# A weight chunk's products with the upper weights first, then those with the lower ones

## The chip, the cores and the metric

The kernel runs on one core of a Trainium2 chip. The core has TensorE for matrix products, VectorE, ScalarE and GpSimd for element-wise work, and SyncE, which here issues the weights' DMAs. The time of a kernel is the device time of the core in microseconds, from a run without the profiler; it is given as a median of several runs. A profile is one more execution, recorded by the hardware profiler, with its own time and, a little shorter, its span from the first to the last instruction.

## The reference

A decoder trunk of two layers on 256 positions of width 2048, all in float32. Layer A mixes positions by attention over three groups of dilated windows. Layer B is an attention of three branches (compressed, selected and sliding-window keys), whose keys and values come from one shared projection. Behind each mixer stand an output projection, a feed-forward part with squared ReLU and a gated embedding; rmsnorms stand ahead of all of them.

```python
qkv = (xn @ w_in).reshape(B, S, 3, G * Hg, dh)           # mixer A
o   = softmax_over_groups(dilated attention) @ w_out
kv  = (hn @ w_kv).reshape(B, S, 6, G, dh)                # shared by mixer B
k_cmp = gelu(blocks(k) @ w1) @ w2                        # compression; v alike
qg  = xn @ w_qg                                          # mixer B: queries, gates
o   = (g0 * o_cmp + g1 * o_slc + g2 * o_win) @ w_out
h   = relu(xn @ mlp_w1) ** 2;   x = x + h @ mlp_w2       # 2048 -> 8192 -> 2048
x   = x + sigmoid(xn @ ple_w_gate) * (p @ ple_w_proj)
```

Nearly all of the arithmetic is in the products of 256 positions with weights.

## The kernel before

The activations are held feature-major: a tile has 128 features on its partitions and the 256 positions on its columns. The products take their operands in a reduced float32 format (fp32r). To keep the precision, each number is split in two: an upper part, which is the number rounded to that format, and a lower part, which is the rest. A split activation tile is 512 columns wide, with the upper halves of the 256 positions in the first 256 columns and the lower halves in the others. The weights are split on the chip too.

The weights come in 875 chunks of 128 by 1024 numbers. For each chunk SyncE issues a DMA to a raw tile (4 buffers), ScalarE casts it to the upper tile `whi` (line 197, 6 buffers), and VectorE subtracts to get the lower tile `wlo` (line 203, 5 buffers). `Program.run` writes the order out by hand: at each chunk it issues the DMAs up to 7 chunks ahead, the casts and subtractions 3 to 4 chunks ahead, then lets the unfinished evictions (Python generators) advance one step each, and then emits the chunk's products. Each engine's queue takes its instructions in the order in which they are written there.

A chunk holds eight weight tiles of 128 by 128. For each of them `mm_tile` issues two products into one PSUM bank: the upper weights with all 512 columns of the split activation (line 321), which gives upper by upper in the first 256 columns and upper by lower in the others, and the lower weights with the first 256 columns (line 322), which adds lower by upper to the first half. Lower by lower is left out. So each of the eight tiles has a product of 512 columns and one of 256, and each product has its own load of 128 by 128 weights into the array. When a bank is complete its two halves are added (`sum_halves`, a copy on ScalarE at line 326 and an addition on VectorE at line 328), or both are added to the residual stream (lines 437 and 438).

Two functions call `mm_tile`. `quad` makes four output tiles of 128 features at once, in four banks. A chunk covers two blocks of 128 input features for these four tiles; eight chunks complete the quad when there are 2048 input features, four chunks when there are 1024, and one chunk for the embedding's 256. Four banks of the ring `mm` and four of the ring `at` take turns between quads. All of the feed-forward part, the gates, the output projections and the shared keys are quads. `single` makes one output tile in one bank from two chunks of eight input blocks each; the queries and keys of mixer A, the queries of mixer B and the last four gate tiles are singles. The very last one sums in 256 columns only (`one_half`, lines 376 to 378) and does not call `mm_tile`.

Three other forms of large product stand beside these. `token_major` makes the value tiles with the activations as the loaded operand and 512 columns of weights streaming (lines 404 to 406, twelve products of 512 columns in a chunk). `compress` has eight products of 256 columns in a chunk (lines 893 and 894); its chunks take turns with those of a value unit. Sixteen products of 512 columns make the gates of mixer B (line 1036).

Of the kernel before, what the change touches and what calls it, by code (L numbers as in the profile page):

```python
# [15 lines left out]
P = 128  # L16
D = 2048
T = 256
KT = D // P
# [113 lines left out]
def kernel(ctx: ExitStack, tc: tile.TileContext, a: dict, out: bass.AP):  # L133
    nc = tc.nc
# [22 lines left out]
    def bank():  # L157
        return pspool.tile([P, 512], F32, tag="mm", name="mm", bufs=4)
# [156 lines left out]
    def have(acts, k):  # L315
        prog.until(lambda: acts[k] is not None)
        return acts[k]

    def mm_tile(ps, hi, lo, col, rhs, first, last):

        nc.tensor.matmul(ps, hi[:, col:col + P], rhs, start=first, stop=False)  # L321
        nc.tensor.matmul(ps[:, :T], lo[:, col:col + P], rhs[:, :T], start=False, stop=last)  # L322

    def sum_halves(ps):
        s = tmp.tile([P, T], F32, tag="es", name="es", bufs=4)
# [7 lines left out]
    def four_banks():  # L333
        parity[0] ^= 1
        if parity[0]:
            return [bank() for _ in range(4)]
        return [p[:, i, :] for p in (banks2(), banks2()) for i in range(2)]

    def delayed(g, n):
        for _ in range(n):  # L340
            yield
        yield from g

    def quad(src, nk, acts, done, hooks=None, single_ring=False, late=False):

        st = []
        for c in range(nk // 2):
            def step(hi, lo, c=c):
                if c == 0:
                    st.extend([bank() for _ in range(4)] if single_ring else four_banks())  # L350
                for i in range(2):
                    have(acts, 2 * c + i)
                for f in range(4):
                    for i in range(2):
                        k = 2 * c + i
                        mm_tile(st[f], hi, lo, i * 512 + f * P, acts[k], k == 0, k == nk - 1)
                if c < nk // 2 - 1:
                    return []
                return [delayed(done(f, st[f]), f // 2 if late else 0) for f in range(4)]
            prog.chunk(src(c), step)  # L360
            for fn in (hooks or {}).get(c, ()):
                prog.op(fn)

    def single(src, acts, done, mid=(), ring=bank, one_half=False):

        st = []
        for c in range(2):
            def step(hi, lo, c=c):
                if c == 0:
                    st.append(ring())  # L370
                for i in range(8):
                    k = 8 * c + i
                    if one_half:
                        xg, ps = have(acts, k), st[0][:, :T]
                        wh, wl = hi[:, i * P:(i + 1) * P], lo[:, i * P:(i + 1) * P]
                        nc.tensor.matmul(ps, wh, xg[:, :T], start=k == 0, stop=False)
                        nc.tensor.matmul(ps, wh, xg[:, T:], start=False, stop=False)
                        nc.tensor.matmul(ps, wl, xg[:, :T], start=False, stop=k == KT - 1)
                        continue
                    mm_tile(st[0], hi, lo, i * P, have(acts, k), k == 0, k == KT - 1)  # L380
                return [done(st[0])] if c else []
            prog.chunk(src(c), step)
            if c == 0:
                for fn in mid:
                    prog.op(fn)
# [902 lines left out]
```

## Time and profile before

| | us |
|---|---|
| median of 3 runs | 2519.74 (2519.64 to 2519.77) |
| profiled execution | 2519.91 |
| its span | 2518.1 |
| TensorE products, busy | 2507.3 |
| TensorE weight loads, busy | 2204.1 |
| VectorE, busy | 1716.8 |
| ScalarE, busy | 1342.8 |
| DMA, mean rate | 185 GB/s |

In the profile, PE is TensorE, PEld its weight loads, DVE is VectorE, ACT is ScalarE, POOL is GpSimd and SP is SyncE. L321 is line 321 of the kernel. A group of instructions is given by line, engine, operation, the written tile, an arrow and the read tiles, with a count, busy time and the mean length of one in ns, and behind the bar the idle time of its engine just before them with what ended it. Products on TensorE are pipelined and their ends are modelled, so a recorded product is longer than the distance to the next one; starts are what counts. A row of the chain has a start, the time that passed until the next link, and the instruction. A row of the windows has the window, its length, the busy time and number of instructions, the granted clock (1.00 is full), the DMA engines' busy share and the rate in GB/s.

### The profile page before, as it was taken

Reading aid. Unit: us, or ns where it says so; the run is one execution under the profiler, and the core shown is the slowest. Engines: PE = TensorE matmul, PEld = TensorE weight load, DVE = VectorE, ACT = ScalarE, POOL = GpSimd, SP = SyncE. Lnnn points to the kernel's source line nnn. Section 1 sums busy time; section 2 is a strip of 40 time slices with the busy share of each in tenths; the row PEclk is TensorE's granted clock in tenths of the full one; section 3 lists DMA queues with packets and bytes.
Section 4 is the critical chain, followed back from the end, with each engine's and each line's share of the span. In section 5 each row is a group of like instructions: output and inputs, shape, how many; then the busy total and the mean of one; then the engine's idle time right before and its main releaser. Section 6 shows DMA issues by size and latency. Waiting matters only on the chain.

```text
span 2518.1 us, 38042 instructions
## 1 busy us (share of the span) xinstructions
PE 2507.3 (100%) x14457; PEld 2204.1 (88%) x14457; DVE 1716.8 (68%) x3000; ACT 1342.8 (53%) x2152; POOL 10.4 (0%) x24
## 2 busy tenths in 40 slices
PE   9999999999999999999999999999999999999998
PEld 8888888888888888888888889888888888888887
DVE  6766677866565665567787989776556656556777
ACT  6444444554454453455564788655435445445555
POOL 0000000000000000000000000000000000000000
PEclk9999999999999999999999999999999999999999
DMA  7555555555555555555565743455555565555653
GB/s 268 173 180 178 175 161 180 176 188 189 193 188 190 192 190 189 190 191 189 185 199 190 248 155 125 141 191 185 192 190 188 191 191 188 190 192 188 190 185 124
DMA packets 130119, 466.23 MB, mean 185 GB/s; under 512 B 14608, under 2 KB 15888, under 8 KB 129936
## 3 DMA queue, kind: packets, MB, share of 16 engines
q1 hardware_dynamic: 129264, 462.68, 56.8%
q8 instruction: 113, 1.85, 0.3%
q0 software_dynamic: 528, 1.07, 0.2%
q14 instruction: 70, 0.57, 0.1%
q10 hardware_dynamic: 144, 0.07, 0.0%
HBM read 461.65 MB, written 2.10 MB: 184 GB/s over the span
## 4 chain that ended last, share of the span: by engine, by line
PE 99%; DVE 0%; DMA 0%; SPq 0%; ACT 0%; issue 0%; DVEq 0%
PE mm L321 31%; PE at L321 26%; PE mm L322 16%; PE at L322 14%; PE mm L404 1%; PE mm L406 1%; PE mm L405 1%; PE at L406 1%; PE at L404 1%; PE at L405 1%; PE at L1135 0%; PE at L673 0%; PE mm L1159 0%; PE mm L893 0%; PE mm L894 0%; DMA raw<-in_w_v 0%
## 5 line engine op out<-in xcount | busy, mean ns | idle before, releaser
L203 DVE TENSOR_TENSOR wlo<-raw,whi 128x1024 fp32r<-128x1024 f32 (+1 forms) x875 | 1065.5, 1219 | 624.8 <-PE at L322 242.1
L197 ACT CAST whi<-raw 128x1024 fp32r<-128x1024 f32 (+1 forms) x875 | 920.4, 1053 | 914.6 <-PE at L321 409.9
L321 PE MATMUL mm<-xa,whi 128*128 128x512 f32 x2176 | 765.1, 395 | 0.0
L322 PE MATMUL mm<-xa,wlo 128*128 128x256 f32 x2176 | 608.1, 279 | 0.0
L321 PE MATMUL at<-xa,whi 128*128 128x512 f32 x1648 | 573.6, 392 | 0.0
L321 PEld LDWEIGHTS mm<-xa,whi 128*128 128x128 f32 x2176 | 407.8, 187 | 91.9 <-issue 0.4
L322 PE MATMUL at<-xa,wlo 128*128 128x256 f32 x1648 | 461.1, 280 | 0.0
L322 PEld LDWEIGHTS mm<-xa,wlo 128*128 128x128 f32 x2176 | 410.6, 189 | 0.4
L321 PEld LDWEIGHTS at<-xa,whi 128*128 128x128 f32 x1648 | 308.3, 187 | 68.0
L321 PE MATMUL at<-h,whi 128*128 128x512 f32 x1024 | 355.7, 391 | 0.0
L321 PE MATMUL mm<-h,whi 128*128 128x512 f32 x1024 | 355.7, 391 | 0.0
L322 PEld LDWEIGHTS at<-xa,wlo 128*128 128x128 f32 x1648 | 311.3, 189 | 0.1
L322 PE MATMUL mm<-h,wlo 128*128 128x256 f32 x1024 | 286.7, 280 | 0.0
L322 PE MATMUL at<-h,wlo 128*128 128x256 f32 x1024 | 286.7, 280 | 0.0
L321 PEld LDWEIGHTS mm<-h,whi 128*128 128x128 f32 x1024 | 191.5, 187 | 42.0
L321 PEld LDWEIGHTS at<-h,whi 128*128 128x128 f32 x1024 | 191.5, 187 | 42.0
L322 PEld LDWEIGHTS mm<-h,wlo 128*128 128x128 f32 x1024 | 193.5, 189 | 0.0
L322 PEld LDWEIGHTS at<-h,wlo 128*128 128x128 f32 x1024 | 193.5, 189 | 0.0
L328 DVE TENSOR_TENSOR et<-mm,es 128x256 f32<-128x256 f32 x137 | 55.8, 422 | 80.3 <-ACT es L326 78.3
L326 ACT COPY es<-mm 128x256 f32<-128x256 f32 x137 | 48.2, 370 | 66.0 <-PE mm L322 63.0
L328 DVE TENSOR_TENSOR et<-at,es 128x256 f32<-128x256 f32 x103 | 43.5, 423 | 36.8 <-ACT es L326 31.3
L326 ACT COPY es<-at 128x256 f32<-128x256 f32 x103 | 37.8, 370 | 51.8 <-DVE et L328 40.5
(301 smaller groups left out, 2387.8 us busy)
## 6 DMA issues: line engine op xcount, KB each, us to landing
raw<-in_w SPq DMA_DIRECT2D x512, 512.0 KB, 3.5
raw<-in_w_qk SPq DMA_DIRECT2D x96, 512.0 KB, 3.7
raw<-in_w_gate SPq DMA_DIRECT2D x56, 512.0 KB, 3.6
raw<-in_w_kv SPq DMA_DIRECT2D x48, 512.0 KB, 4.2
raw<-in_w_v SPq DMA_DIRECT2D x46, 512.0 KB, 3.6
raw<-in_w_q SPq DMA_DIRECT2D x32, 512.0 KB, 4.4
raw<-in_w_oB SPq DMA_DIRECT2D x32, 512.0 KB, 3.6
raw<-in_w_oA SPq DMA_DIRECT2D x16, 512.0 KB, 3.6
```

The source lines that it names most:

```text
L197: nc.scalar.copy(hi[:, c], t[:, c])
L203: nc.vector.tensor_sub(lo[:, c], t[:, c], f32(hi)[:, c])
L321: nc.tensor.matmul(ps, hi[:, col:col + P], rhs, start=first, stop=False)
L322: nc.tensor.matmul(ps[:, :T], lo[:, col:col + P], rhs[:, :T], start=False, stop=last)
L326: nc.scalar.copy(s, ps[:, :T])
L328: nc.vector.tensor_add(t, ps[:, T:], s)
L404: nc.tensor.matmul(st[j], xh, wh, start=k == 0, stop=False)
L405: nc.tensor.matmul(st[j], xl, wh, start=False, stop=False)
L406: nc.tensor.matmul(st[j], xh, wl, start=False, stop=k == KT - 1)
```

## The change

`mm_tile` becomes `mm_tiles`, which takes the chunk's list of eight weight tiles. It issues the eight products with the upper weights (512 columns each), and then the eight with the lower weights (256 columns each). Within each group the order of the tiles is that of before. `quad` and `single` hand it the list; the last single, `token_major`, `compress` and the gates stay as they are. No product is added or left out, and the sums in each PSUM bank get the same terms in another order.

```diff
-    def mm_tile(ps, hi, lo, col, rhs, first, last):
-        nc.tensor.matmul(ps, hi[:, col:col + P], rhs, start=first, stop=False)
-        nc.tensor.matmul(ps[:, :T], lo[:, col:col + P], rhs[:, :T], start=False, stop=last)
+    def mm_tiles(hi, lo, tiles):
+        for ps, col, rhs, first, last in tiles:
+            nc.tensor.matmul(ps, hi[:, col:col + P], rhs, start=first, stop=False)
+        for ps, col, rhs, first, last in tiles:
+            nc.tensor.matmul(ps[:, :T], lo[:, col:col + P], rhs[:, :T], start=False, stop=last)
...
-                for f in range(4):
-                    for i in range(2):
-                        k = 2 * c + i
-                        mm_tile(st[f], hi, lo, i * 512 + f * P, acts[k], k == 0, k == nk - 1)
+                mm_tiles(hi, lo, [(st[f], i * 512 + f * P, acts[2 * c + i], 2 * c + i == 0, 2 * c + i == nk - 1)
+                                  for f in range(4) for i in range(2)])
...
+                tiles = []
                 for i in range(8):
...
-                    mm_tile(st[0], hi, lo, i * P, have(acts, k), k == 0, k == KT - 1)
+                    tiles.append((st[0], i * P, have(acts, k), k == 0, k == KT - 1))
+                mm_tiles(hi, lo, tiles)
```

In the changed kernel the two products stand on lines 326 and 328.

## The prediction

> **What bounds the kernel now.** I read the page first (busy time, slices, chain), then the windows of the two changed lines, then the chain of work piece by piece where single products can be timed.
>
> ```profile
> PE 2507.3 (100%) x14457; PEld 2204.1 (88%) x14457; DVE 1716.8 (68%) x3000; ACT 1342.8 (53%) x2152; POOL 10.4 (0%) x24
> PEclk9999999999999999999999999999999999999999
> PE mm L321 31%; PE at L321 26%; PE mm L322 16%; PE at L322 14%; PE mm L404 1%; PE mm L406 1%; PE mm L405 1%; PE at L406 1%; PE at L404 1%; PE at L405 1%; PE at L1135 0%; PE at L673 0%; PE mm L1159 0%; PE mm L893 0%; PE mm L894 0%; DMA raw<-in_w_v 0%
> L321 PE MATMUL mm<-h,whi 128*128 128x512 f32 x1024 | 355.7, 391 | 0.0
> L328 DVE TENSOR_TENSOR et<-mm,es 128x256 f32<-128x256 f32 x137 | 55.8, 422 | 80.3 <-ACT es L326 78.3
> L326 ACT COPY es<-mm 128x256 f32<-128x256 f32 x137 | 48.2, 370 | 66.0 <-PE mm L322 63.0
> L203 DVE TENSOR_TENSOR wlo<-raw,whi 128x1024 fp32r<-128x1024 f32 (+1 forms) x875 | 1065.5, 1219 | 624.8 <-PE at L322 242.1
> L197 ACT CAST whi<-raw 128x1024 fp32r<-128x1024 f32 (+1 forms) x875 | 920.4, 1053 | 914.6 <-PE at L321 409.9
> ```
>
> TensorE is the bound: it is busy for 2507 of 2518 us at an undiminished clock, and 87% of the chain is lines 321 and 322, the two that move. The makers of the split weights wait for TensorE to free their buffers, not the reverse: VectorE's subtraction and ScalarE's cast of line 203 and 197 idle mostly on a product of line 322 or 321. So an earlier or later wait on a weight tile is worth little, and what counts is how long TensorE takes from the start of one product to the start of the next.
>
> ```profile
> 0.00:2518.10 2518.10, 2204.75 (x6320) 1.00 0.57 185
> ```
>
> This is the window over the whole span for line 321 alone (busy time, and products in brackets). A wide product's recorded time (391 ns in the group row above) is longer than a pair's spacing, so the busy time is one cover over all unbroken stretches of pairs: 6320 pairs, or 790 chunks of 8, in 2204.75 us. Each of the program's 77 stretches is counted about 0.04 too long (0.39 against 0.35), 3 us together, which leaves 2201 us, or 2.787 us a chunk.
>
> ```profile
> 599.80 0.23 PE mm L321
> ...
> 606.04 0.23 PE at L321
> ```
>
> ```profile
> 40.81 0.23 PE mm L321
> ...
> 44.34 0.24 PE mm L321
> ```
>
> Both are the chain (start, length, product). In the MLP, 18 pairs take 606.04 - 599.80 = 6.24 us: 0.3467 a pair, 2.773 a chunk. In the first head's single tiles 10 pairs take 3.53: 0.353 a pair, 2.824 a chunk, with the same products. The spacing thus has a steady value and a slower one, into which a stretch can fall and stay. Over 790 chunks the clean value gives 2191 us, so some 10 us of the 2201 are slow stretches and slow restarts after other TensorE work.
>
> **The change, part by part.**
>
> What is issued. Nothing is added or removed: the same 6320 products with the upper and 6320 with the lower weights, and one weight load for each, as now (14457 loads for 14457 products). In the built program the instructions of VectorE, ScalarE, GpSimd and SyncE stand in the same order as before, DMAs too; only TensorE's order differs, and two more separate waits stand in its queue. So the sum is about spacing. Before, a chunk alternates 512 and 256 columns wide; after, eight products of 512 are followed by eight of 256, and the next chunk goes back to 512.
>
> Spacing in long rows of one width. The row of pairs is not the only form in this trace.
>
> ```profile
> 79.82 0.23 PE mm L405
> ...
> 85.94 0.23 PE mm L405
> ```
>
> ```profile
> 2498.86 0.12 PE at L376
> ...
> 2499.81 0.12 PE at L378
> ...
> 2501.01 0.12 PE at L376
> ```
>
> Twenty-seven products of 512 of a value unit take 6.12 us: 0.2267 each. Ten products of 256 of the last tile, 2499.81 to 2501.01, take 1.20: 0.120 each. Together 0.3467, the same as a clean pair. So a long row of one width gains nothing and loses nothing against clean alternation: this term is 0.
>
> The turn from one width to the other. Where the compression and a value unit take turns, chunks of eight 256-wide and twelve 512-wide products already alternate, all products one after another:
>
> ```profile
> 1400.58 0.23 PE at L404
> ...
> 1419.15 0.23 PE at L404
> ...
> 1431.04 0.23 PE at L404
> ...
> 1432.20 0.23 PE at L406
> ...
> 1433.79 0.12 PE mm L893
> ...
> 1434.75 0.23 PE at L404
> ```
>
> Twelve wide ones take 2.75 us where 12 x 0.2267 = 2.720; the first five take 1.16 where the steady rate gives 1.133, and from there on they run steadily. Eight narrow ones take 0.96, as 8 x 0.120. Five whole periods, from 1400.58 to 1419.15, take 18.57 us, 3.714 each, so a turn to and fro costs 3.714 - 3.680 = 0.034 us, nearly all in the first five wide products after a turn and at the last. The changed chunk makes exactly this turn once: eight wide are more than the five that are slow, so it pays in full. 790 x 0.034 = +27 us. Bounds: 0 (no such cost in this form) and 0.045 (next row).
>
> The form itself. Only one row of wide products with weights as the loaded operand and activations streaming exists, the gates:
>
> ```profile
> 1460.00 0.23 PE mm L321
> 1460.24 0.12 PE mm L322
> 1460.35 3.71 PE mm L1036 x16
> ```
>
> Sixteen in 3.71 us are 0.232 each: they never reach 0.2267. It stands amid slow pairs (1460.00 to 1460.35 is 0.35 for one and the neighbours are 0.353), so I take the row with the same alternation of widths, the compression's, and keep this one as the upper end.
>
> Slow stretches that go. The turn sets the spacing anew in every chunk, so a slow stretch can't last. Of the 10 us above clean, about half are restarts, which stay: a first pair after transposes has 0.31 between its two products where 0.23 is usual,
>
> ```profile
> 1607.37 0.47 PE L321 MATMUL mm<-ko,whi 128*128 128x512 f32 x1
> 1607.68 0.28 PE L322 MATMUL mm<-ko,wlo 128*128 128x256 f32 x1
> ```
>
> and there are dozens of such restarts. The other half, 5 to 6 us, is replaced by the turn's price. Bounds 0 and 10; I take -6.
>
> Waits. The lower weights' tile is asked for at the ninth product, about 8 x 0.23 - 0.23 = 1.6 us later than now; the upper tile is free 16 x 0.173 - 8 x 0.23, some 0.9 us, sooner. TensorE hardly waits for either now (longest wait on line 203: 0.4 us, once), so 0.
>
> ```profile
> PE at L406 <- DVE wlo L203: 0.4, 1, 0.4
> ```
>
> Evictions. In a quad's last chunk the four banks are now complete at 0.69, 1.39, 2.08 and 2.77 us of the chunk; after, at about 2.1, 2.3, 2.6 and 2.8. Four sums that were spread come in a bunch, and VectorE and ScalarE hold a cast or subtraction behind them. What hides it: those tiles are made three chunks (8 us) ahead, the other four banks serve the next quad, and eight chunks (22 us) pass before a bank returns. Without that cover it would be up to 2 us for a quad, four copies of 0.37 and four adds of 0.42, less what overlaps. In the four quads of one chunk the next quad has eight chunks. A single tile's one bank ends when it did. I take 0.
>
> Activations. The eighth activation of a single tile is needed 7 x 0.12 = 0.8 us earlier; they were split chunks before. 0.
>
> Sum: +27 - 6 = +21 us on the profiled execution, 2519.91 us with a span of 2518.1 (the windows' row above has that span); the median of the runs is 2519.74, 0.2 less. Forecast 2540.5 us, +0.8%. With the two terms at their bounds, 2536 to 2549.
>
> **The rivals.**
>
> Rates add. If the turn costs nothing with weights loaded and activations streaming, a chunk is 8 x 0.2267 + 8 x 0.120 = 2.773, as clean now. For it: the clean rates sum exactly. Against it: the compression's period. Time: 2519.7 less 0 to 6 us for slow stretches, about 2517, no measurable change. The Trainium skill, "TensorE: Matmul & The Clock Gate", section "Back-to-back issue gap", gives a spacing of N/2.4 + 2.5 ns, with no term for order, thus 8 x 215.8 + 8 x 109.2 = 2.600 us a chunk before and after and no change; the trace's clean 2.773 shows that something is missing in it, the turns in the compression that order can matter.
>
> Narrow products run faster after a turn. The first eight of line 376 after the pairs take 2499.81 - 2498.86 = 0.95, 0.01 below the steady rate. If each chunk got that and the wide ones were steady at once: 8 x 0.2267 + 0.95 = 2.763. 790 x (2.763 - 2.773) = -8, with the slow stretches -14: 2506 us. It decides if the wide start costs under 0.01. For it: this one row; against: the eight narrow ones in the compression show 0.96.
>
> Wide products never settle. At the gates' 0.232 a chunk is 8 x 0.232 + 0.96 = 2.816, +0.043 on the clean one: +34 - 6 = +28, 2548 to 2549 us. For: the same operand roles. Against: its slow surroundings.
>
> The bunch of sums delays a cast enough that TensorE waits. 0.5 us on each of 76 or so quads would be 38 us. Against: eight microseconds of lead and VectorE at 68%.
>
> **How the numbers follow.** Turn as in the compression 0.44; rates add 0.22; narrow faster 0.14; never settle 0.16; bunched sums 0.04. A measurement here tells about 0.2% (5 us) from no change: faster than 2514.7, 0.14 + 0.06 of the second case; within, 0.16; slower, 0.44 + 0.16 + 0.04. The range 2509 to 2552 leaves out the case of 2506 and the fourth rival; the forecast's own range is 2536 to 2549.
>
> **What would show it.** Right: in the chain of the MLP, eight wide products after a narrow one take 1.84 to 1.85 us (not 1.81), the next eight 0.96, a chunk 2.80 to 2.81; the cover of line 321's and 328's products grows by some 21 us, all elsewhere unchanged; VectorE and ScalarE keep their busy time. Wrong: a chunk of 2.77 (rates add), of 2.76 or less, or waits of TensorE for line 203 or 197.

## The result and the profile after

The changed kernel takes 2532.06 us (median, 2531.84 to 2532.27) against 2519.76 us for the kernel before in the same comparison: a ratio of 1.0049, interval 1.0038 to 1.0059. It is slower by 12.3 us, as forecast in sign; 2540.5 was forecast, with 2536 to 2549 as the forecast's own range. The profiled execution took 2532.27 us with a span of 2530.5.

The page of the profile after, the lines that answer to those shown of before:

```profile
PE 2518.4 (100%) x14457; PEld 2212.9 (87%) x14457; DVE 1709.0 (68%) x3000; ACT 1337.2 (53%) x2152; POOL 10.5 (0%) x24
PEclk9999999999999999999999999999999999999999
L203 DVE TENSOR_TENSOR wlo<-raw,whi 128x1024 fp32r<-128x1024 f32 (+1 forms) x875 | 1064.4, 1218 | 579.2 <-PE at L328 219.5
L197 ACT CAST whi<-raw 128x1024 fp32r<-128x1024 f32 (+1 forms) x875 | 916.1, 1049 | 808.8 <-PE at L326 380.8
```

The counts and the clock are the same, and VectorE and ScalarE still wait for TensorE. The chain of the MLP shows the spacing (equal products that follow each other are merged, with their count):

```profile
599.79 1.61 PE mm L326 x7
601.40 0.95 PE mm L328 x8
602.35 1.84 PE at L326 x8
604.19 0.95 PE at L328 x8
605.14 0.93 PE at L326 x4
```

Eight wide products take 1.84 us and eight narrow ones 0.95, 2.79 for the chunk where it was 2.773. The single starts give 2.7933: the wide ones stand at 233, 236, 228, 233, 231, 227, 227 and 227 ns from one start to the next, the narrow ones at 113, 119 and six times 120. So the wide row pays 27 ns above eight times 226.7, in its first five, and the first two narrow ones give 7 back: 20 ns a chunk. The chunk of 2.793 lies between the 2.77 that was to refute the forecast and the 2.80 to 2.81 that was to confirm it.

Where the pairs had run slowly, rows are faster. In the first head's single tiles a chunk of pairs took 2.82 to 2.83; after:

```profile
41.11 1.84 PE mm L326 x8
42.95 0.95 PE mm L328 x8
43.91 1.84 PE mm L326 x8
```

that is 43.91 - 41.11 = 2.80, 2.793 by the starts, the same as in the MLP. Summed over all chunks, from the first start of a chunk to the start of what follows its last product, in us:

| stage | chunks | before | after |
|---|---|---|---|
| heads of mixer A | 96 | 270.37 | 270.27 |
| output projection A | 16 | 44.68 | 44.32 |
| MLP 0 | 256 | 710.52 | 715.36 |
| gated embedding 0 | 36 | 100.28 | 101.79 |
| shared keys | 32 | 89.13 | 89.66 |
| heads of mixer B | 32 | 91.22 | 90.68 |
| output projection B | 32 | 90.60 | 90.43 |
| MLP 1 | 256 | 710.53 | 715.34 |
| gated embedding 1 | 34 | 94.73 | 96.19 |
| all | 790 | 2202.06 | 2214.05 |

The 12.0 us of the last line are the measured difference. The two MLPs bring 9.7 of them, 19 ns a chunk. The gated embeddings bring 3.0, and two thirds of that are waits that were not there before. The waits of TensorE in the profile after (us in total, times, longest), and the chain around the second of these places:

```profile
PE at L326 <- DVE x L444: 0.7, 2, 0.4
```

```profile
2415.56 1.22 DVE wlo L203
2416.78 0.35 DVE x L443
2417.12 0.02 issue
2417.15 0.43 DVE x L444
2417.57 0.34 DVE x L443
2417.91 0.02 issue
2417.94 0.43 DVE x L444
2418.37 0.14 issue
2418.51 1.17 PE at L326 x4
```

The last quad of the MLP, just ahead of the embedding, now completes its four banks in a bunch. Its eight additions to the residual (lines 443 and 444) stand on VectorE with a subtraction among them, and TensorE's chain passes through them: the gate's first quad wants those banks again after one embedding quad of a single chunk. That first gate chunk takes 3.42 us in the one layer and 3.41 in the other, in place of 2.77. Two more chunks, each behind an embedding quad (near 1235 and 2444 us), take 3.13. There the sums are not late. The last of the quad before, an addition on VectorE, ends at 1236.02, 1.03 us after the gate chunk's start (1234.99); in the kernel before it was 1.04 us (1230.92 and 1229.88). The rows, after and before:

```profile
1235.60 0.42 DVE L334 TENSOR_TENSOR et<-at,es 128x256 f32<-128x256 f32 x1 [0.44 <-ACT es L332]
```

```profile
1230.50 0.42 DVE L328 TENSOR_TENSOR et<-at,es 128x256 f32<-128x256 f32 x1 [0.44 <-ACT es L326]
```

But a row of wide products comes to the second pair of banks sooner: after four of them, 0.93 us, where the alternating order needed four pairs, 1.39 us. TensorE's chain is interrupted just there:

```profile
1235.15 0.93 PE at L326 x4
1236.08 0.09 issue
1236.17 1.17 PE at L326 x4
```

Behind the MLPs both things act. The last addition ends 1.3 us after the chunk's start, where it was 0.4 to 0.5 before, and the row asks at 0.93. Where the second pair is asked for late again, none of the four chunks waits: with rows of four (below) it comes after four wide and four narrow products, 1.41 us, and the four chunks take 2.81 each.

### The profile page after: what moved, and what is told of

It reads as the page before. It is cut to its first block, busy times and chain, and to the rows that moved or that the text cites. A ratio compares the mean times of both kernels' runs of the same rounds, so it can differ in the third digit from the quotient of the medians.

```text
span 2530.5 us, 38028 instructions
## 1 busy us (share of the span) xinstructions
PE 2518.4 (100%) x14457; PEld 2212.9 (87%) x14457; DVE 1709.0 (68%) x3000; ACT 1337.2 (53%) x2152; POOL 10.5 (0%) x24
## 4 chain that ended last, share of the span: by engine, by line
PE 98%; DVE 1%; DMA 0%; ACT 0%; SPq 0%; issue 0%; DVEq 0%
PE mm L326 31%; PE at L326 26%; PE mm L328 16%; PE at L328 13%; PE mm L410 1%; PE mm L412 1%; PE mm L411 1%; PE at L412 1%; PE at L410 1%; PE at L411 1%; PE at L1141 0%; PE at L679 0%; PE mm L1165 0%; PE mm L899 0%; PE mm L900 0%; DMA raw<-in_w_v 0%
## 5 line engine op out<-in xcount | busy, mean ns | idle before, releaser
L326 PE MATMUL mm<-xa,whi 128*128 128x512 f32 x2176 | 548.3, 394 | 0.0
L326 PE MATMUL at<-xa,whi 128*128 128x512 f32 x1648 | 414.4, 393 | 0.9 <-DVE x L444 0.7
L328 PEld LDWEIGHTS mm<-xa,wlo 128*128 128x128 f32 x2176 | 296.8, 190 | 21.4
L328 PE MATMUL mm<-xa,wlo 128*128 128x256 f32 x2176 | 303.3, 282 | 0.0
L326 PE MATMUL mm<-h,whi 128*128 128x512 f32 x1024 | 256.4, 392 | 0.0
L326 PE MATMUL at<-h,whi 128*128 128x512 f32 x1024 | 256.4, 392 | 0.0
L328 PEld LDWEIGHTS at<-xa,wlo 128*128 128x128 f32 x1648 | 224.8, 190 | 16.1
L328 PE MATMUL at<-xa,wlo 128*128 128x256 f32 x1648 | 229.8, 282 | 0.0
L328 PE MATMUL mm<-h,wlo 128*128 128x256 f32 x1024 | 142.8, 282 | 0.0
L328 PE MATMUL at<-h,wlo 128*128 128x256 f32 x1024 | 142.8, 282 | 0.0
```

## The experiments

My theory was that the price lies in the turn from a narrow to a wide row. The rivals were a price for the chunk (the lower tile asked for late, the sums that come in a bunch), and a price of the weights' order itself, whatever the widths.

**Rows of four and of two.** The eight tiles are taken in groups; n is 4 or 2. In this edit and the following ones `wide` issues one tile's product of 512 columns and `narrow` its product of 256.

```diff
-        for ps, col, rhs, first, last in tiles:
...
+        for b in range(0, 8, n):
+            for t in tiles[b:b + n]:
+                wide(hi, t)
+            for t in tiles[b:b + n]:
+                narrow(lo, t)
```

> Four upper products, then four lower ones, twice in a chunk: two turns from narrow to wide in place of one. If the cost sits in the turn (the changed kernel's MLP chunk is 2.793 us against 2.773, with all of the surplus in the first five wide products), each turn costs 15 to 20 ns, since a row of four wide ones ends before the slow start does: chunk 2.80 to 2.81, time 2541 to 2547 us. If the cost is one for the chunk, whatever the order inside (another wait, a change of weight tile, sums that come late), the time stays at 2532.

> Two upper, two lower products, four times in a chunk. If every turn pays 8 (what the first two wide products of a row showed, less the gain at the first narrow one) to 20 ns: chunk 2.805 to 2.853, 2541 to 2582 us. If the cost grows with the length of a row and a short row has none, as rows of one have none: 2.773 to 2.78, 2520 to 2525 us.

Measured: 2538.95 us for rows of four, 1.0076 (1.0061 to 1.0091) of before, and 2524.94 us for rows of two, 1.0021 (1.0011 to 1.0030). The chain of the first, then of the second:

```profile
596.21 0.93 PE mm L321 x4
597.14 0.47 PE mm L325 x4
597.61 0.93 PE mm L321 x4
598.54 0.48 PE mm L325 x4
599.02 0.93 PE mm L321 x4
```

```profile
597.42 0.46 PE mm L321 x2
597.89 0.23 PE mm L325 x2
598.12 0.47 PE mm L321 x2
598.59 0.23 PE mm L325 x2
598.82 0.46 PE mm L321 x2
```

Two turns in a chunk cost 34 ns (599.02 - 596.21 = 2.81; 2.8067 by the starts), 17 for each; the one turn of the changed kernel costs 20. So the price is not one for the chunk. The chunk is as expected, the time 2 us below the expected range. Rows of two have four turns and pay 13 ns in all (2.787 by the starts), 3 for each: a chunk between the two that were expected, and a time at the upper end of the second range. The turn's price grows with the length of the rows on both sides and is nearly complete at four.

**Half the turns.** Odd chunks take the lower weights first, so rows of 16 stand across two chunks.

```diff
+    def mm_tiles(hi, lo, tiles, c):
+        for t in tiles if c % 2 == 0 else ():
+            wide(hi, t)
+        for t in tiles:
+            narrow(lo, t, c % 2 == 0)
+        for t in tiles if c % 2 else ():
+            wide(hi, t, True)
```

> Even chunks upper first, odd chunks lower first: rows of 16, and half the turns. The turn as the cause gives half the price, 10 ns a chunk: 2.783 in the MLP and about 2524 us in all. A price for the chunk (a second tile asked for, late sums, the change of operand) gives 2532 again.

Measured: 2524.35 us, 1.0018 (1.0009 to 1.0027), as expected of the turn. Its chain shows where the price is paid:

```profile
597.09 1.91 PE mm L325 x16
599.00 1.84 PE mm L321 x8
600.84 1.81 PE at L321 x8
602.66 1.91 PE at L325 x16
```

The eight wide products behind the sixteen narrow ones take 1.84 us, the eight behind those 1.81. By the starts, chunks take 2.801 and 2.766 in turn, 2.783 on average: 10 ns above a clean chunk of pairs, half of the changed kernel's 20.

**Width or weights.** The lower weights get all 512 columns, too, so that nothing is narrow, once in the order of before and once in rows.

```diff
-            nc.tensor.matmul(ps[:, :T], lo[:, col:col + P], rhs[:, :T], start=False, stop=last)
+            nc.tensor.matmul(ps, lo[:, col:col + P], rhs, start=False, stop=last)
```

> The lower weights, too, take all 512 columns (this adds the lower by lower product, which the reference's split leaves out), in the alternating order of before. Sixteen products at 0.2267 are 3.627 us a chunk, 2866 us for 790, 3184 us in all. It is the first half of a pair with wide_rows.

> The same products (lower by lower is added here, too), eight upper, then eight lower, as in the changed kernel. If the change of width costs, there is none here, and it takes as long as wide_alt, within 3 us. If the change from upper to lower weights in rows costs, or the late request of the lower tile, or the bunched sums, it takes 12 us more than wide_alt, as the changed kernel does against the one before.

Measured, in one execution each: 3191.73 us alternating and 3192.69 us in rows. The chunks sum to 2875.1 and 2875.8 us, and 688 of the 790 take 3.627 in both. Lower weights in a row, asked for later, completing their banks later, cost under 1 us without a change of width. This separates the width from the rest.

**Late sums.** In each quad's last chunk the products alternate as before.

```diff
+    def mm_tiles(hi, lo, tiles, n):
+        for b in range(0, 8, n):
+            for t in tiles[b:b + n]:
+                wide(hi, t)
+            for t in tiles[b:b + n]:
+                narrow(lo, t)
...
-                                  for f in range(4) for i in range(2)])
+                                  for f in range(4) for i in range(2)], 1 if c == nk // 2 - 1 else 8)
```

> Upper first, but in each quad's last chunk the products alternate as before, so that its four banks are complete one after another. If late sums cost nothing but the five chunks that wait for a bank (at 1208, 1235, 2417 and 2444 us of the span and near 1600), those 2 to 3 us come back, and the 76 chunks or so that alternate save 20 ns each, 1.5 us: 2528 us. If the bunched sums were the main cost: 2520 us.

Measured: 2532.73 us, 1.0051 (1.0036 to 1.0066), no gain: a miss. The waits behind the MLPs are gone (the first gate chunks take 2.82 us in place of 3.4). The two behind the embedding quads stay (3.14 and 3.16 near 1235 and 2444 us), as they come from the early request and not from late sums, and the quads' last chunks, 91 by their count and not 76, took more time where they were to save 20 ns:

```profile
599.60 0.23 PE mm L321
599.84 0.12 PE mm L325
599.96 0.24 PE mm L321
600.20 0.12 PE mm L325
600.32 0.23 PE mm L321
...
602.44 1.82 PE at L321 x8
604.26 0.95 PE at L325 x8
```

From 599.60 to 602.44 the chunk takes 2.84 (2.831 or 2.832 by the starts), the slow spacing of pairs. Pairs that begin behind a row of narrow products fall into the slow spacing, not the clean one; the row behind them then pays 18 less (2.775). What the late sums cost was got back, about 1.2 us, and lost again here.

**Quads alone, single tiles alone.** With the same function, rows of eight in the one and of one, that is pairs, in the other.

```diff
-                                  for f in range(4) for i in range(2)])
+                                  for f in range(4) for i in range(2)], 8)
...
-                mm_tiles(hi, lo, tiles)
+                mm_tiles(hi, lo, tiles, 1)
```

This is quads_only; in singles_only the 8 and the 1 change places.

> Upper first in the quads alone, alternating in the single tiles. By the stages' sums of the two profiles (heads of mixer A 270.37 us before and 270.27 after, heads of mixer B 88.29 and 88.39) the single tiles take the same time in both orders, so 2532 us. If the single tiles' eight products into one bank have a price of their own: different by over 1 us.

> Upper first in the single tiles alone. By the same sums 2519.8 us, within 0.5. The reason would be two effects that cancel: 20 ns a chunk more where the alternating pairs ran clean, 20 to 40 less where they had fallen into the slow spacing.

Measured: 2532.91 us, 1.0053 (1.0037 to 1.0070), and 2519.41 us, 0.9998 (0.9989 to 1.0008). The whole difference is in the quads; in the single tiles the two effects nearly cancel. For the heads of mixer B the expectation's sums (88.29 and 88.39) are not those of the table above, which has 91.22 before and 90.68 after; rows gain 0.1 us in the heads of mixer A and 0.5 in those of B.

**The place of the operands.** One stage of the changed kernel did not fit. In the output projection of mixer A its chunks take less than a clean chunk of pairs:

```profile
456.66 1.83 PE at L326 x8
458.49 0.91 PE at L328 x8
459.40 1.83 PE at L326 x8
```

456.66 to 459.40 are 2.74; by the starts chunks of 2.741 and 2.773 alternate. The products are those of the MLP, but the activations (oT) start 64 bytes past the weights' place modulo 512 bytes, while xa and h in the kernels above start at the weights' own place (addresses of the built program). Two runs moved the tiles by putting unused ones between them and left the order as it was; the first edit stands in the changed kernel (rows_off64), the second, which moves all tiles at once, in the kernel before (pairs_pad96).

```diff
+    ctx.enter_context(tc.tile_pool(name="padw", bufs=1)).tile([P, 16], F32, name="padw")
     wpool = ctx.enter_context(tc.tile_pool(name="w", bufs=4))
+    ctx.enter_context(tc.tile_pool(name="padh", bufs=1)).tile([P, 16], F32, name="padh")
```

```diff
+    ctx.enter_context(tc.tile_pool(name="padc", bufs=1)).tile([P, 24], F32, name="padc")
     const = ctx.enter_context(tc.tile_pool(name="const", bufs=1))
```

> The changed kernel with 64 bytes more ahead of the weight tiles and 64 more behind them, so that activations (xa, h) and weights no longer start at the same place modulo 128 bytes; nothing else moves. In the changed kernel's output projection of mixer A the activations lie like that, and its chunks take 2.741 and 2.773 us in turn, 2.757 on average, against 2.793 elsewhere. If the place of the operands sets the spacing: 2.757 in the MLP too, and 790 x 0.036 = 28 us less, 2504 us. If it is the state that the projection started in, or the four chunks of its quads: 2532 us as before.

> The kernel before with 96 bytes ahead of everything, so that all large tiles start at a multiple of 64 bytes (they start 32 past one now) while weights and activations keep their distance. If only the distance between the two matters: 2519.8 us, and 2.773 a chunk. If the place of each counts, as a read that starts between two lines of 64 bytes would: less than 2.773 a chunk, down to 2.62 without any surplus over the columns' time of 0.2133 and 0.1067, which would be 2400 us; I expect 2.773.

Measured: 2516.04 us, 0.9986 (0.9976 to 0.9995), for the rows, and 2519.57 us, 1.0000 (0.9990 to 1.0009), for the pairs. A shift that pairs' operands have in common plays no part, so the expectation's rival for pairs falls (its two figures make 2.56 a chunk, not 2.62). Rows change with the distance, but the full 28 us did not come: h stood 64 past the weights and its chunks take 2.741 and 2.773 in turn; xa stood 64 short of them, and its chunks take 2.773. So the second pair of runs put both 64 past, with 448 bytes ahead of the weights: rows_at64 is the changed kernel with it, pairs_at64 the one before.

```diff
+    ctx.enter_context(tc.tile_pool(name="padw", bufs=1)).tile([P, 112], F32, name="padw")
     wpool = ctx.enter_context(tc.tile_pool(name="w", bufs=4))
+    ctx.enter_context(tc.tile_pool(name="padh", bufs=1)).tile([P, 16], F32, name="padh")
```

> The changed kernel with 448 bytes more ahead of the weight tiles and 64 behind them: xa and h both start 64 bytes past the weights' place, modulo 512. In the changed kernel oT stood like that, and with the last placement h did, and both took 2.757 us a chunk; xa, 64 bytes short of the weights' place, took 2.773. If the distance sets the price: 2.757 in all of the MLP, 514 chunks of which about half were at 2.773 so 4 us less than 2516.0, and up to 3 us less in the singles: 2509 to 2513 us, faster than the kernel before. If xa's chunks have another reason: 2516.

> The kernel before, alternating, with the same placement. Its chunks on oT, 64 bytes past the weights' place, took 2.791 us where those on xa and h took 2.773. If the distance sets the price of either order, the MLP goes to 2.791: 514 x 0.018 = 9 us more there, 2524 to 2534 us in all, so that the rows would be the faster order by 0.5 to 1%. If the placement helps every order alike: below 2519.7.

Measured: 2510.92 us, 0.9963 (0.9950 to 0.9975), for the rows: faster than both kernels. The pairs take 2547.66 us, 1.0108 (1.0093 to 1.0124), slower in sign as expected, but 14 us above the expected range: the first MLP ran at the 2.791 a chunk that was expected, the second at 2.826. That it is the distance and not the place itself is borne out by h: in rows_off64 and rows_at64 it starts 64 past the weights at different addresses, and its chunks take 2.741 and 2.773 in turn in both.

The same runs hold one more distance. In both placements oT comes to lie 128 bytes past the weights (by the same addresses); there rows take 2.80 and 2.82 us in turn in place of 2.741 and 2.773, and pairs 2.81 in place of 2.791. And at 64 past, products of one width are slowed too: in wide_alt the chunks on oT take 3.66 us, those of the MLP 3.627. Windows of 100 us in the two MLPs, with the number of products, for the kernel before, the changed one, rows_at64 and pairs_at64:

```profile
600.00:700.00 100.00, 100.00 (x579) 1.00 0.59 189
2000.00:2100.00 100.00, 100.00 (x579) 1.00 0.59 188
```

```profile
600.00:700.00 100.00, 100.00 (x576) 1.00 0.63 189
2000.00:2100.00 100.00, 100.00 (x576) 1.00 0.63 190
```

```profile
600.00:700.00 100.00, 100.00 (x581) 1.00 0.62 192
2000.00:2100.00 100.00, 100.00 (x581) 1.00 0.60 192
```

```profile
600.00:700.00 100.00, 100.00 (x575) 1.00 0.60 189
2000.00:2100.00 100.00, 100.00 (x568) 1.00 0.59 185
```

With activations and weights at the same place pairs do 579 and rows 576; 64 bytes apart rows do 581 and pairs 575, or 568 in the second MLP, where they ran in the slow spacing of 2.826 on average. Which order is the faster one depends on where the tiles lie.

## Why the prediction was right, and where its sizes were off

What bounds the kernel: right. TensorE's clock, its count and the other engines' work stayed, and only its spacing moved.

Long rows of one width cost nothing: right where the operands lie at the same place. 226.7 and 120 ns are reached again in the second half of each row, and without a change of width the two orders are equal (3.627 a chunk in both).

The turn, predicted at 34 ns from the compression's period, is right as a mechanism and was mis-sized: 20 ns, 15.8 us over 790 chunks in place of 27. The wide half was the same (the first five take 1.16 us in the compression and in the changed kernel). The difference is at the other end of the row: in the compression the last wide and the first narrow product stand at 233 and 124 ns, in the changed kernel at 227 and 113. The two forms differ in which operand is loaded and in where their tiles lie; the placement runs show that the place alone can move a chunk by 20 to 36 ns, but which of the two made these 14 was not tried. The bounds of 0 and 45 held it.

The sign is in part luck. The price came from a form whose operands lie elsewhere, and the prediction did not ask where they lie. At the kernel's own placement a turn costs 20 ns; with xa and h 64 bytes past the weights the same order is faster than pairs at either placement, and the forecast would have had the wrong sign.

Slow stretches, taken at -6: 12.0 = 15.8 + 2.0 - x gives x = 5.8, right in size. This x is what is left over, not a count of slow chunks. By the table 3.2 of it are in the heads, where it more than pays for 2.6 us of turns; 0.7 is in output projection A, where the place makes rows fast and not the end of a slow stretch.

Evictions, taken at 0: wrong by about 2 us (the four chunks take 0.65, 0.36, 0.64 and 0.36 us more than before). This miss hid a part of the turn's, which was 11 us too large. The step said that four quads of one chunk are followed by eight chunks, and so have time. It overlooked the quad on the other side: the gate behind the embedding's one chunk takes the banks of the quad before it, 2.8 us after they are complete, not 22. And it looked at when the banks are complete, not at when they are asked for: a row asks for its second pair of banks 0.46 us sooner than pairs do, which alone makes two of the four waits. Where a ring of banks is short, the shortest quad in it sets the time to clear, not the typical one.

Waits and activations at 0: right; TensorE waits for line 203 once, 0.5 us, as it did before for 0.4.

The range: the forecast's own, 2536 to 2549, was missed by 4 us; the wide one, 2509 to 2552, held. The own range is called that of the two terms at their bounds and is not: 0 to 0.045 us a chunk and 0 to 10 us of slow stretches make 2510 to 2555.

The rivals: "rates add" fell by the runs above. The Trainium skill's page "TensorE: Matmul & The Clock Gate", section "Back-to-back issue gap", has a gap of N/2.4 + 2.5 ns without a term for order, from which the prediction took an estimate of 2.600 us a chunk; the page calls it the isolated gap, and for streams with a weight load for each product it gives about 131 ns at N=512. The runs agree with neither: rows of 512 take 226.7 ns a product. Chunks of the same products, free of waits, take from 2.741 to 2.832 us, by order, by place and by what ran before. "Narrow products run faster after a turn" is true of the first two (113 and 119 ns) and does not outweigh the wide ones. "Never settle" did not happen; at the kernel's own placement wide rows settle in five. "The bunch of sums" does not show where it was feared, at the casts: TensorE waits for a weight tile as little as before.

## What to carry to other kernels

On a TensorE-bound kernel with 100% busy time the distance from start to start is the thing to read: take it for each sequence of widths, find the same sequence elsewhere in the trace, and price a reordering by that, not by the lengths of single products. Before a neighbour's price is taken over, compare both ends of its rows and where its operands lie. And when an order of products is judged, try it at a second placement: 512 bytes of padding, which set xa and h 64 bytes past the weights, turned a loss of 0.5% here into a gain of 0.4%.

## What was not expected of the hardware

The distance between the starts of the streamed and the loaded operand's tiles sets TensorE's spacing, as far as these runs go: with rows, 2.793 us a chunk at the same place, 2.773 at 64 bytes short, 2.757 at 64 past and 2.81 at 128 past; with pairs, 2.773 at the same place, 2.791 or 2.826 at 64 past and 2.81 at 128 past. A shift of all by 96 bytes changed nothing for pairs (2519.57 us); with rows it was not tried. What in the memory or in TensorE makes this was not found. The distances of 128 stand on one stage of 16 chunks, and no run was made for others.

The spacing also has a memory. Pairs at the same place run at 2.773 or at up to 2.832 a chunk, and stay in either until something else runs on TensorE; a row of narrow products ahead of them led into the slow one. At 64 past, too, the same order on the same distances ran at 2.791 in one MLP and at 2.826 in the other. How a stretch falls into one or the other stays open.
